# Down projection by one level of Strassen's algorithm, in three chunks of the depth

## The chip, the core and the metric

The kernel runs on one core of a Trainium2 chip. The metric is device time in microseconds (us), the median of several executions; lower is better. Besides the executions that are only timed, one is profiled, and all rows below come from that one.

## The reference, cut to what matters

The program is a trunk layer: a token mixer (a state-space branch and an mLSTM branch), then a feed-forward block. The change lies in the last matrix product of the feed-forward block.

```python
def channel_mixer(x, g_pre, g_post, w_gate, w_up, w_conv, b_conv, w_down):
    h = rmsnorm(x, g_pre)
    a = causal_dwconv(h @ w_gate, w_conv, b_conv)
    y = (jax.nn.gelu(a, approximate=True) * (h @ w_up)) @ w_down
    return x + rmsnorm(y, g_post)
```

There are 2048 tokens after the 16 meta tokens are dropped, D = 1024 and FFN_DIM = 2816, so the down projection is a 2048 x 2816 by 2816 x 1024 product, in float32 accuracy.

## The kernel before, in words

Every float32 product is made of three matmuls: each operand is split into a rounded part "hi" (ScalarE, ACT, a copy into the fp32r type) and a remainder "lo" (VectorE, DVE, a subtraction), and `mm3` (lines 155 to 158) or `mm3x` (160 to 163, the same with the group check off) adds hi*hi, hi*lo and lo*hi in PSUM. A matmul has a 128 x 128 stationary operand and up to 512 moving columns.

The order of the work on each engine is made by a scheduler when the program is built: it takes instructions in the order of the program as far as their inputs and buffers are there, and may move later ones ahead. All transfers are issued from the SP queue, in the order so found.

The stages around the change:

- **The gate and up products (FFN stage).** They are already done by one level of Strassen's algorithm, in two halves of the tokens, p = 0 and p = 1. `ops_first` (1050) and `ops_second` (1066) make the seven combinations of the moving operand from the normalised activations: `op_load` brings two of the four blocks for two of the four depth tiles (1 MB each, into a buffer of the tag `mk`, of which there are three), three subtractions form the combinations in place, and `op_split` (1045) makes hi and lo. The results lie in the buffers `t4(0)` to `t4(11)` and `q4(0)`, `q4(1)`, of which there is one each. `ffn_weights` (1131) loads the gate and up weights of one 128-column block m, forms the combinations `s1` to `s4` and splits seven of them with `put` (lines 1142, 1143). `ffn_unit` (1163) runs the seven products in the order 1, 6, 2, 7, 5, 4, 3 in the PSUM tiles A, B and C; DVE or ACT reads a sum out between two products that follow each other in the same tile (`u1`, `u2`, `u3`, lines 1184 to 1204). Then come the convolution (1220 to 1222), the GELU and the product, and `y` goes to the DRAM buffer `y_d` (1228). A halo of two columns is copied between the halves by GpSimd (POOL, line 1168).
- **Between the halves** (1236, 1237) the moving operands of p = 1 are made, in the same buffers as those of p = 0.
- **The down projection** (1245 to 1295). For each half `nh` of the 1024 output columns, all 22 depth tiles of `w_down` are loaded and split (1257 to 1265), 22 x 2 buffers of 512 columns in `t4(0)` to `t4(10)`. For each of 16 token tiles, `y` comes back from `y_d` in three pieces (1271), is split (1274, 1275) and used as the stationary operand: 22 x 3 matmuls of 512 columns in one PSUM tile. ACT sums the squares (1281); DVE multiplies by the gain `g4b`, and in the second half normalises, adds the residual `h1_d` (1291, 1294) and the result is stored (1295). `rstd_of` (101) takes the inverse root on POOL.

Of the kernel before, what the change touches and what calls it, by code (L numbers as in the profile page):

```python
# [49 lines left out]
def mixer_ffn_kernel(  # L50
# [32 lines left out]
    y_d = dp.tile([NF, 128, 2048], F32, name="y_d")  # L83
    win_d = dp.tile([8, 128, 512], F32, name="win_d")
# [947 lines left out]
    WX = (514, 512)  # L1032

    def op_load(p, hf, half):
        w = WX[p]
        t = mk_tile()[:, 0:4 * w].rearrange("p (k c) -> p k c", k=2)
        ks = slice(4 * half + 2 * hf, 4 * half + 2 * hf + 2)
        if p == 0:
            G.memset(t[:, :, 0:2], 0.0)
            P.dma_start(out=t[:, :, 2:2 * w], in_=h2_d[:, ks, 14:14 + 2 * w - 2])  # L1040
        else:
            P.dma_start(out=t, in_=h2_d[:, ks, 1040:1040 + 2 * w])
        return t[:, :, 0:w], t[:, :, w:2 * w]

    def op_split(op, p, hf, src):
        hi, lo = (o[:, 2 * hf:2 * hf + 2, 0:WX[p]] for o in op)
        S.activation(hi, src, AF.Copy)  # L1047
        V.tensor_tensor(lo, src, hi.bitcast(F32), ALU.subtract)  # L1048

    def ops_first(p):  # L1050

        op = {n: (t4(2 * i), t4(2 * i + 1)) for i, n in enumerate((1, 6, 2, 7))}
        for hf in range(2):
            b11, b12 = op_load(p, hf, 0)
            op_split(op[1], p, hf, b11)
            b21, b22 = op_load(p, hf, 1)
            E = V if p else G
# [3 lines left out]
            op_split(op[6], p, hf, b22)  # L1061
            op_split(op[2], p, hf, b21)
            op_split(op[7], p, hf, b12)
        return op

    def ops_second(p, op, last):

        op.update({5: (t4(8), t4(9)), 4: (t4(10), t4(11)), 3: last()})
        for hf in range(2):
            b11, b12 = op_load(p, hf, 0)  # L1070
            b21, b22 = op_load(p, hf, 1)
            V.tensor_tensor(b11, b12, b11, ALU.subtract)
            op_split(op[5], p, hf, b11)
            V.tensor_tensor(b12, b22, b11, ALU.subtract)
            V.tensor_tensor(b21, b21, b12, ALU.subtract)
            op_split(op[4], p, hf, b21)
            op_split(op[3], p, hf, b22)
# [33 lines left out]
    op0 = ops_first(0)  # L1111
# [19 lines left out]
    def ffn_weights(m):  # L1131

        wg = dw.tile([128, D], F32, tag="ws", name="wg")
        P.dma_start(out=wg, in_=w_gate[m])
        wu = dw.tile([128, D], F32, tag="ws", name="wu")
        P.dma_start(out=wu, in_=w_up[m])
        a11, a12, a21, a22 = wg[:, 0:512], wg[:, 512:D], wu[:, 0:512], wu[:, 512:D]
        out_ = {}

        def put(n, pl, tag, src):  # L1140
            t = pl.tile([128, 2, 512], F32R, tag=tag, name=f"w{n}")
            S.activation(t[:, 0], src, AF.Copy)  # L1142
            V.tensor_tensor(t[:, 1], src, t[:, 0].bitcast(F32), ALU.subtract)  # L1143
            out_[n] = t.rearrange("p a (k f) -> p a k f", k=4)

        s1 = du.tile([128, 512], F32, tag="s1", name="s1")
        s2 = du.tile([128, 512], F32, tag="s2", name="s2")
        s3 = du.tile([128, 512], F32, tag="s3", name="s3")
# [9 lines left out]
        s4 = du.tile([128, 512], F32, tag="s3", name="s4")  # L1158
        V.tensor_tensor(s4, a12, s2, ALU.subtract)
        put(3, dx, "w3", s4)  # L1160
        return out_

    def ffn_unit(p, m, op):
# [8 lines left out]
        def piece(p0, pn):  # L1172


            def prod(ps, n, first):
                for k in range(4):
                    mm3x(ps, wt[n][:, 0, k], wt[n][:, 1, k], op[n][0][:, k, p0:p0 + pn], op[n][1][:, k, p0:p0 + pn],
                         first and k == 0, k == 3)

# [4 lines left out]
            prod(A, 1, True)  # L1184
            S.activation(u1, A, AF.Copy)
            yield
            prod(B, 6, True)
            V.tensor_tensor(u2, B, u1, ALU.add)
            yield
            prod(A, 2, False)  # L1190
            S.activation(gp_[:, x0 + p0:x0 + p0 + pn], A, AF.Copy)
            yield
            prod(B, 7, False)
# [3 lines left out]
            prod(C, 5, True)  # L1197
            V.tensor_tensor(u3, C, u3, ALU.add)
            yield
            prod(B, 4, False)  # L1200
            V.tensor_tensor(u1, B, u1, ALU.add)
            yield
            prod(C, 3, False)
# [14 lines left out]
        for o0, o1 in ((0, xe), (xe, 1024)):  # L1218
            c = dx.tile([128, 514], F32, tag="cc", name="cc", bufs=3)[:, 0:o1 - o0]
# [10 lines left out]
    ops_second(0, op0, lambda: (q4(0), q4(1)))  # L1230
# [5 lines left out]
    op1 = ops_first(1)  # L1236
    ops_second(1, op1, lambda: (q4(0), q4(1)))
    for m in range(NF):
        ffn_unit(1, m, op1)
    phX.close()  # L1240
    el = pool(ctx, "el", bufs=2)
# [5 lines left out]
    g4b = el.tile([128, D], F32, name="g4b", bufs=1)  # L1247
    bcast_row(g4b, g_ffn_post)
    o4 = [t4(11).bitcast(F32), q4(0).bitcast(F32), q4(1).bitcast(F32), el.tile([128, 4, 514], F32, name="o4", bufs=1)]
    o0 = [o4[i // 4][:, i % 4, 0:512] for i in range(16)]  # L1250
    sq2 = [el.tile([128, 2], F32, name=f"sq_{i}", bufs=1) for i in range(16)]
    chunks = [(0, 8), (8, 8), (16, 6)]
    for nh in range(2):
        wd = {}
        for k in range(0, NF, 4):
            kn = min(4, NF - k)
            w_s = mk_tile()[:, 0:kn * 512].rearrange("p (a n) -> p a n", a=kn)
            P.dma_start(out=w_s, in_=w_down[k * 128:(k + kn) * 128, nh * 512:(nh + 1) * 512].rearrange(
                "(a p) n -> p a n", a=kn))
            for a in range(kn):  # L1260
                if a % 2 == 0:
                    t = t4((k + a) // 2)
                wh, wl = wd[k + a] = (t[:, a % 2 * 2, 0:512], t[:, a % 2 * 2 + 1, 0:512])
                S.activation(wh, w_s[:, a], AF.Copy)
                V.tensor_tensor(wl, w_s[:, a], wh.bitcast(F32), ALU.subtract)
        for i in range(16):
            ps = pst("ac", [128, 512])
            for k0, kn in chunks:
                r = "p (m t) -> p m t"
                ys = dw.tile([128, D], F32, tag="ws", name="ys")[:, 0:kn * 128]  # L1270
                P.dma_start(out=ys.rearrange(r, m=kn),
                            in_=y_d[k0:k0 + kn, :, i * 128:(i + 1) * 128].rearrange("m p t -> p m t"))
                yh, yl = (dw.tile([128, D], F32R, tag=tg, name="yhl")[:, 0:kn * 128] for tg in ("wh", "wl"))
                S.activation(yh, ys, AF.Copy)  # L1274
                V.tensor_tensor(yl, ys, yh.bitcast(F32), ALU.subtract)  # L1275
                yh, yl = yh.rearrange(r, m=kn), yl.rearrange(r, m=kn)
                for kk in range(kn):
                    k = k0 + kk
                    mm3(ps, yh[:, kk], yl[:, kk], wd[k][0], wd[k][1], k == 0, k == NF - 1)
            jk = el.tile([128, 512], F32, tag="jk", name="jk")  # L1280
            S.activation(jk, ps, AF.Square, accum_out=sq2[i][:, nh:nh + 1])
            if nh == 0:
                V.tensor_tensor(o0[i], ps, g4b[:, 0:512], ALU.mult)
            else:
                o1 = el.tile([128, 512], F32, tag="o1", name="o1")
# [88 lines left out]
```

## Time and profile before

| what | value |
|---|---|
| median of 3 executions (lowest, highest) | 2879.54 us (2877.54, 2880.41) |
| the profiled execution: its time, its span | 2886.44 us, 2884.7 us |
| PE busy, share of the span | 2794.8 us, 97% |
| DVE, ACT, POOL busy | 1798.8, 1047.4, 183.2 us |
| FFN stage, p = 1, and its boundary from p = 0 | about 1945 to 2381 us |
| down projection, first and last matmul | 2381.0 and 2877.3 us |

The span runs from the first to the last instruction of the profiled execution; its time as the other executions are timed is 1.7 us more. "Busy" is the time in which an engine has an instruction in work. Matmuls overlap in the pipeline, so that the length of one says less than the distance from one start to the next.

### The profile page before, as it was taken

The numbers are of one execution on the slowest core, as the hardware profiler recorded it, in microseconds if no ns is written. First come the engines' busy times: TensorE is split into PE (matmuls) and PEld (weight loads), VectorE is DVE, ScalarE is ACT, GpSimd is POOL, SyncE is SP. The second block draws the span as 40 slices with busy tenths as digits, with TensorE's granted clock in tenths as the row PEclk, the third lists the DMA queues.
The fourth block names the chain that finished last, engine by engine and source line by source line (L and its number), as shares of the span: only waits on it lengthen the run. The fifth ranks groups of instructions, "written<-read, shape, count | busy, mean of one in ns | idle before, by whom it ended". The sixth has DMA issues, their size and how long they took to land.

```text
span 2884.7 us, 41374 instructions
## 1 busy us (share of the span) xinstructions
PE 2794.8 (97%) x15654; PEld 2506.7 (87%) x15654; DVE 1798.8 (62%) x3508; ACT 1047.4 (36%) x1995; POOL 183.2 (6%) x257
## 2 busy tenths in 40 slices
PE   8999999999999999998779999998999999999999
PEld 8999999999999987776579999996888888888887
DVE  4638897377555465576777777788777774224333
ACT  6102233233443444434344444444444443223221
POOL 1000000000000000212310000001000000000000
PEclk9999999999999999999989999999999999999999
DMA  8334453211454564676746222224222235334553
GB/s 303 105 73 137 169 162 117 74 69 70 147 158 134 159 200 134 196 221 219 234 142 201 80 81 84 71 82 175 81 84 78 87 98 179 95 99 146 166 168 125
DMA packets 328442, 389.74 MB, mean 135 GB/s; under 512 B 41569, under 2 KB 230390, under 8 KB 328114
## 3 DMA queue, kind: packets, MB, share of 16 engines
q1 hardware_dynamic: 328242, 387.10, 41.9%
q8 instruction: 123, 2.02, 0.3%
q14 instruction: 77, 0.63, 0.1%
HBM read 282.90 MB, written 104.12 MB: 134 GB/s over the span
## 4 chain that ended last, share of the span: by engine, by line
PE 83%; DMA 7%; DVE 6%; issue 2%; ACT 1%; POOL 1%; SPq 0%; POOLq 0%; DVEq 0%; ACTq 0%
PE mm L158 9%; PE mm L156 9%; PE mm L157 9%; PE ac L157 8%; PE ac L158 8%; PE ac L156 8%; PE ac L162 5%; PE ac L163 5%; PE ac L161 5%; PE mm L163 4%; PE mm L162 4%; PE mm L161 4%; DMA mk<-h_d 1%; DMA wo_d<-W 1%; DMA h_d<-mk 1%
## 5 line engine op out<-in xcount | busy, mean ns | idle before, releaser
L158 PE MATMUL mm<-hTh,wl 128*128 128x410 f32 (+3 forms) x1216 | 430.4, 354 | 0.0
L156 PE MATMUL mm<-hTh,wh 128*128 128x410 f32 (+3 forms) x1216 | 429.4, 353 | 0.1
L157 PE MATMUL mm<-hTl,wh 128*128 128x410 f32 (+3 forms) x1216 | 427.2, 351 | 0.0
L1275 DVE TENSOR_TENSOR yhl<-ys,yhl 128x1024 fp32r<-128x1024 f32 (+1 forms) x96 | 109.1, 1137 | 293.7 <-ACT yhl L1274 293.7
L157 PE MATMUL ac<-t,yhl 128*128 128x512 f32 x704 | 278.5, 396 | 0.0
L158 PE MATMUL ac<-t,yhl 128*128 128x512 f32 x704 | 277.3, 394 | 0.0
L156 PE MATMUL ac<-t,yhl 128*128 128x512 f32 x704 | 276.6, 393 | 0.0
L161 PE MATMUL mm<-t,w 128*128 128x258 f32 (+2 forms) x792 | 254.6, 322 | 12.6 <-ACT w L1142 9.7
L161 PE MATMUL ac<-t,w 128*128 128x258 f32 (+2 forms) x792 | 255.0, 322 | 12.1 <-ACT t L1047 8.0
L162 PE MATMUL mm<-t,w 128*128 128x258 f32 (+2 forms) x792 | 255.1, 322 | 1.3 <-DVE t L1048 1.3
L162 PE MATMUL ac<-t,w 128*128 128x258 f32 (+2 forms) x792 | 254.9, 322 | 1.1 <-DVE t L1048 1.1
L163 PE MATMUL mm<-t,w 128*128 128x258 f32 (+2 forms) x792 | 253.6, 322 | 1.7 <-DVE w L1143 1.7
L163 PE MATMUL ac<-t,w 128*128 128x258 f32 (+2 forms) x792 | 254.7, 322 | 0.0
L140 ACT ACTIVATE wh<-ws 128x512 fp32r<-128x512 f32 (+1 forms) x176 | 124.5, 708 | 317.7 <-PE mm L157 139.3
L156 PEld LDWEIGHTS mm<-hTh,wh 128*128 128x128 f32 x1216 | 229.2, 188 | 3.2 <-DVE ev L351 0.8
L157 PEld LDWEIGHTS mm<-hTl,wh 128*128 128x128 f32 x1216 | 229.2, 189 | 2.6
L158 PEld LDWEIGHTS mm<-hTh,wl 128*128 128x128 f32 x1216 | 229.2, 189 | 2.4
L1274 ACT ACTIVATE yhl<-ys 128x1024 fp32r<-128x1024 f32 (+1 forms) x96 | 94.8, 988 | 350.6 <-PE ac L157 349.0
L1142 ACT ACTIVATE w<-s 128x512 fp32r<-128x512 f32 x176 | 110.3, 630 | 192.5 <-PE ac L163 112.3
L161 PEld LDWEIGHTS mm<-t,w 128*128 128x128 f32 x792 | 151.0, 191 | 25.6 <-ACT w L1142 9.9
L161 PEld LDWEIGHTS ac<-t,w 128*128 128x128 f32 x792 | 150.7, 190 | 25.1 <-ACT t L1047 8.3
L142 DVE TENSOR_TENSOR wl<-ws,wh 128x512 fp32r<-128x512 f32 (+1 forms) x112 | 104.5, 936 | 108.4 <-ACT wh L140 108.1
(448 smaller groups left out, 6180.2 us busy)
## 6 DMA issues: line engine op xcount, KB each, us to landing
ys<-y_d SPq DMA_DIRECT2D x64, 512.0 KB, 3.7
wg<-in_w_gate_dram SPq DMA_DIRECT2D x44, 512.0 KB, 4.8
wu<-in_w_up_dram SPq DMA_DIRECT2D x44, 512.0 KB, 3.9
gab_d<-ev SPq DMA_DIRECT2D x80, 205.0 KB, 2.2
ws<-in_w_m_dram SPq DMA_DIRECT2D x32, 512.0 KB, 4.0
ws<-in_w_out_dram SPq DMA_DIRECT2D x64, 256.0 KB, 3.0
gat<-gab_d SPq DMA_DIRECT2D x48, 256.0 KB, 3.6
ys<-y_d SPq DMA_DIRECT2D x32, 384.0 KB, 3.1
```

The lines of the kernel that those rows point to most:

```text
L140: S.activation(wh, ws, AF.Copy, scale=scale)
L142: V.tensor_tensor(wl, ws, wh.bitcast(F32), ALU.subtract)
L156: T.matmul(out=ps, lhsT=lh, rhs=rh, start=first, stop=False)
L157: T.matmul(out=ps, lhsT=lh, rhs=rl, start=False, stop=False)
L158: T.matmul(out=ps, lhsT=ll, rhs=rh, start=False, stop=last)
L161: T.matmul(out=ps, lhsT=lh, rhs=rh, start=first, stop=False, skip_group_check=True)
L162: T.matmul(out=ps, lhsT=lh, rhs=rl, start=False, stop=False, skip_group_check=True)
L163: T.matmul(out=ps, lhsT=ll, rhs=rh, start=False, stop=last, skip_group_check=True)
L1142: S.activation(t[:, 0], src, AF.Copy)
L1274: S.activation(yh, ys, AF.Copy)
L1275: V.tensor_tensor(yl, ys, yh.bitcast(F32), ALU.subtract)
```

## The change

The down projection is done by the same scheme as the gate and up products. The depth of 22 tiles is cut into three chunks of 6, 8 and 8 tiles (each two halves of 3, 4 and 4). In each chunk, blocks of `w_down` are the moving operands, made by the same `ops_first` and `ops_second` (both load the blocks anew), with the subtractions on DVE; pairs of token tiles of `y` are the stationary operands, made by `stationary`, which is `ffn_weights` without its loads. A chunk has eight units of seven products. The output of a unit is four tiles of 512 columns, `a`, in a buffer of the tag `mk`; it is stored to `acc_d` after the first chunk, loaded, added to and stored in the second, and loaded, added to and normalised in the third. The old functions are made general and keep their work; the buffer tag "cc" has four buffers in place of three, and the pools of the FFN stage stay open.

```diff
+    acc_d = dp.tile([8, 128, 2048], F32, name="acc_d")
...
+    def ops_first(load, nk, w, E):
 
         op = {n: (t4(2 * i), t4(2 * i + 1)) for i, n in enumerate((1, 6, 2, 7))}
+        for k in range(0, nk, 2):
+            n = min(2, nk - k)
+            b11, b12 = load(0, k, n)
+            op_split(op[1], w, k, n, b11)
+            b21, b22 = load(1, k, n)
             E.tensor_tensor(b11, b12, b11, ALU.subtract)
             E.tensor_tensor(b12, b22, b12, ALU.subtract)
             E.tensor_tensor(b22, b22, b11, ALU.subtract)
+            op_split(op[6], w, k, n, b22)
+            op_split(op[2], w, k, n, b21)
+            op_split(op[7], w, k, n, b12)
         return op
 
+    def ops_second(load, nk, w, op, last):
 
         op.update({5: (t4(8), t4(9)), 4: (t4(10), t4(11)), 3: last()})
+        for k in range(0, nk, 2):
+            n = min(2, nk - k)
+            b11, b12 = load(0, k, n)
+            b21, b22 = load(1, k, n)
             V.tensor_tensor(b11, b12, b11, ALU.subtract)
+            op_split(op[5], w, k, n, b11)
             V.tensor_tensor(b12, b22, b11, ALU.subtract)
             V.tensor_tensor(b21, b21, b12, ALU.subtract)
+            op_split(op[4], w, k, n, b21)
+            op_split(op[3], w, k, n, b22)
...
+    g4b = du.tile([128, 1028], F32, tag="gp", name="g4b")[:, 0:D]
     bcast_row(g4b, g_ffn_post)
-    for nh in range(2):
...
-        for i in range(16):
-            ps = pst("ac", [128, 512])
...
-                    mm3(ps, yh[:, kk], yl[:, kk], wd[k][0], wd[k][1], k == 0, k == NF - 1)
...
+    def wd_load(k0, nk):
+        def load(half, k, n):
+            t = mk_tile()[:, 0:n * D].rearrange("p (k c) -> p k c", k=n)
+            r0 = (k0 + half * nk + k) * 128
+            P.dma_start(out=t, in_=w_down[r0:r0 + n * 128, :].rearrange("(k p) n -> p k n", k=n))
+            return t[:, :, 0:512], t[:, :, 512:D]
+        return load
+
+    def y_pair(k0, nk, i):
+        yr = []
+        for half in range(2):
+            t = dw.tile([128, 4, 256], F32, tag="ws", name="yr")[:, 0:nk]
+            m0 = k0 + half * nk
+            P.dma_start(out=t, in_=y_d[m0:m0 + nk, :, i * 256:(i + 1) * 256].rearrange("m p t -> p m t"))
+            yr.append(t)
+        return stationary(yr[0][:, :, 0:128], yr[1][:, :, 0:128], yr[0][:, :, 128:256], yr[1][:, :, 128:256])
+
+    def down_unit(c, nk, wt, op, i):
+        a = mk_tile()[:, 0:2048].rearrange("p (a n) -> p a n", a=4)
+        if c:
+            P.dma_start(out=a.rearrange("p a n -> p (a n)"), in_=acc_d[i])
...
+        def more(j, u):
+            if c == 0:
+                return u
+            G.tensor_tensor(a[:, j], a[:, j], u, ALU.add)
+            return a[:, j]
+
+        prod(A, wt, op, 1, nk, pc, True)
+        S.activation(u1, A, AF.Copy)
+        prod(B, wt, op, 6, nk, pc, True)
+        V.tensor_tensor(u2, B, u1, ALU.add)
+        a12 = more(1, u2)
+        prod(A, wt, op, 2, nk, pc, False)
+        if c:
+            V.tensor_tensor(a[:, 0], A, a[:, 0], ALU.add)
+        else:
+            S.activation(a[:, 0], A, AF.Copy)
+        prod(B, wt, op, 7, nk, pc, False)
+        V.tensor_tensor(u3, B, u1, ALU.add)
+        a22 = more(3, u3)
+        a21 = more(2, u1)
+        C = pst("ac", [128, 512])
+        prod(C, wt, op, 5, nk, pc, True)
+        V.tensor_tensor(a[:, 3], C, a22, ALU.add)
+        prod(B, wt, op, 4, nk, pc, False)
+        V.tensor_tensor(a[:, 2], B, a21, ALU.add)
+        prod(C, wt, op, 3, nk, pc, False)
+        V.tensor_tensor(a[:, 1], C, a12, ALU.add)
+        if c < 2:
+            P.dma_start(out=acc_d[i], in_=a.rearrange("p a n -> p (a n)"))
+            return
+        for j in (1, 0):
...
+                P.dma_start(out=ht, in_=h1_d[NM + ts.start:NM + ts.stop, hh * 512:(hh + 1) * 512])
...
+                S.activation(jk, a[:, 2 * j + hh], AF.Square, accum_out=sq2[:, hh:hh + 1])
+                (V if i == 7 else G).tensor_tensor(a[:, 2 * j + hh], a[:, 2 * j + hh],
+                                                   g4b[:, hh * 512:(hh + 1) * 512], ALU.mult)
...
+            rs = rstd_of(dsm, sq, 128, 1, 1.0 / D)
+            for hh, ht in enumerate(hts):
+                V.scalar_tensor_tensor(ht, a[:, 2 * j + hh], rs, ht, ALU.mult, ALU.add)
+                P.dma_start(out=out[ts, hh * 512:(hh + 1) * 512], in_=ht)
+
+    for c, (k0, nk) in enumerate(((0, 3), (6, 4), (14, 4))):
+        ld = wd_load(k0, nk)
+        op = ops_first(ld, nk, 512, V)
+        ops_second(ld, nk, 512, op, lambda: (q4(0), q4(1)))
+        for i in range(8):
+            down_unit(c, nk, y_pair(k0, nk, i), op, i)
```

## Rows read from the trace of the kernel before

**Rows 1.** The page: busy time of PE, and shares of the last chain.

```profile
PE 2794.8 (97%) x15654; PEld 2506.7 (87%) x15654; DVE 1798.8 (62%) x3508; ACT 1047.4 (36%) x1995; POOL 183.2 (6%) x257
...
PE 83%; DMA 7%; DVE 6%; issue 2%; ACT 1%; POOL 1%; SPq 0%; POOLq 0%; DVEq 0%; ACTq 0%
```

**Rows 2.** Windows: us, PE, PEld, DVE, ACT, POOL busy (instructions), PEclk, DMA share, GB/s.

```profile
1953.00:1961.50 8.50, 0.49 (x1) 0.19 (x1) 7.38 (x12) 3.28 (x6) 6.38 (x1) 0.76 0.58 213
1961.50:1968.00 6.50, 6.49 (x16) 5.09 (x17) 6.50 (x7) 2.06 (x3) 0.00 (x0) 0.53 0.23 89
...
2100.00:2200.00 100.00, 100.00 (x432) 80.98 (x431) 73.43 (x116) 42.83 (x67) 6.08 (x5) 1.00 0.26 87
2381.00:2400.00 19.00, 19.00 (x83) 15.36 (x82) 16.31 (x25) 11.03 (x18) 0.49 (x1) 1.00 0.89 296
...
2500.00:2600.00 100.00, 100.00 (x432) 80.88 (x431) 26.26 (x26) 22.87 (x32) 0.00 (x0) 1.00 0.32 92
```

**Rows 3.** Groups by line: one of the three matmul lines of the down projection.

```profile
L157 PE MATMUL ac<-t,yhl 128*128 128x512 f32 x704 | 278.5, 396 | 0.0
```

**Rows 4.** Timeline of PE between the halves: the first and the last wait.

```profile
1946.16 0.50 PE L162 MATMUL mm<-t,w 128*128 128x512 f32 x1 [1.31 <-DVE t L1048]
...
1961.51 1.22 PE L161 MATMUL ac<-t,w 128*128 128x512 f32 x2 [8.01 <-ACT t L1047]
```

**Rows 5.** The chain in order of time, between the halves: start, us, what.

```profile
1918.89 0.44 DVE u L1201
...
1953.29 6.38 POOL gp L1168
```

**Rows 6.** Groups by line: operand splits of 1024 columns, and the normalising step of 512.

```profile
L1048 DVE TENSOR_TENSOR t<-mk,t 128x1024 fp32r<-128x1024 f32 x12 | 14.5, 1220 | 1.4 <-ACT t L1047 1.4
L1047 ACT ACTIVATE t<-mk 128x1024 fp32r<-128x1024 f32 x12 | 12.4, 1051 | 1.4 <-DVE mk L1060 1.2 <-DVE mk L1059 0.2
...
L1294 DVE SCALAR_TENSOR_TENSOR ht<-o,rs,ht 128x512 f32<-128x512 f32 x20 | 14.6, 747 | 2.9 <-POOL rs L105 2.9
```

**Rows 7.** Timeline of DVE with full work: start, us.

```profile
1956.53 1.22 DVE L1048 TENSOR_TENSOR t<-mk,t 128x1024 fp32r<-128x1024 f32 x1
1957.66 0.69 DVE L1143 TENSOR_TENSOR w<-wg,w 128x512 fp32r<-128x512 f32 x1
1958.26 0.69 DVE L1151 TENSOR_TENSOR s<-s,wg 128x512 f32<-128x512 f32 x1
```

**Rows 8.** DMA issues from 1900 to 2000 us: count, KB each, us to landing.

```profile
mk<-h_d SPq DMA_DIRECT2D x5, 1024.0 KB, 6.2
mk<-in_w_down_dram SPq DMA_DIRECT2D x3, 1024.0 KB, 4.9
wu<-in_w_up_dram SPq DMA_DIRECT2D x5, 512.0 KB, 4.0
```

**Rows 9.** Timelines of POOL and of DVE, where POOL adds tiles of 512 columns.

```profile
1190.25 3.44 POOL L1021 TENSOR_TENSOR o<-o,xh 128x512 f32<-128x512 f32 x2 [1.00 <-DVE o L1020]
...
1197.50 1.31 POOL L1021 TENSOR_TENSOR o<-o,xh 128x512 f32<-128x512 f32 x1 [0.72 <-DMA xh<-in_x_dram]
...
1190.82 1.73 DVE L142 TENSOR_TENSOR wl<-ws,wh 128x512 fp32r<-128x512 f32 x1
...
1195.57 1.77 DVE L142 TENSOR_TENSOR wl<-ws,wh 128x512 fp32r<-128x512 f32 x1
1198.73 0.69 DVE L142 TENSOR_TENSOR wl<-ws,wh 128x512 fp32r<-128x512 f32 x1 [1.40 <-ACT wh L140]
```

**Rows 10.** SP at the stores of y: waits in ns, min/median/max.

```profile
L1228 SPq EVENT_SEMAPHORE  x81: 17/17/10147, 1510.8 to 2371.7; - x81
```

**Rows 11.** Timeline of the end: last matmul, square, last stores.

```profile
2877.29 0.39 PE L158 MATMUL ac<-t,yhl 128*128 128x512 f32 x1
2877.71 0.60 ACT L1281 ACTIVATE jk<-ac 128x512 f32<-128x512 f32 x1 [9.14 <-PE ac L158]
...
2880.88 0.99 SPq L1295 DMA_DIRECT2D out_dram<-ht  x2
```

More of the change, by code (lines that the diff above doesn't have):

```diff
@@ L1026, in norm_block, with op_split @@
             norm_tile(mk_tile(), pl, blkC[b][0] + c0, rows)
[L1032 to L1046, printed above, removed]
+    def op_split(op, w, k, n, src):
+        hi, lo = (o[:, k:k + n, 0:w] for o in op)
         S.activation(hi, src, AF.Copy)
         V.tensor_tensor(lo, src, hi.bitcast(F32), ALU.subtract)
-    def ops_first(p):
+    def ops_first(load, nk, w, E):
         op = {n: (t4(2 * i), t4(2 * i + 1)) for i, n in enumerate((1, 6, 2, 7))}
[L1053 to L1057, printed above, removed]
+        for k in range(0, nk, 2):
[3 more added lines that the diff above has]
+            b21, b22 = load(1, k, n)
             E.tensor_tensor(b11, b12, b11, ALU.subtract)
@@ L1129, in mixer_ffn_kernel, with stationary @@
     dsm = Small(dx, "n", 2)
[L1131 to L1137, printed above, removed]
+    def stationary(a11, a12, a21, a22):
+        nk = a11.shape[1]
         out_ = {}
         def put(n, pl, tag, src):
[L1141 to L1148, printed above, removed]
+            t = pl.tile([128, 2, 4, 128], F32R, tag=tag, name=f"w{n}")
+            S.activation(t[:, 0, 0:nk], src, AF.Copy)
+            V.tensor_tensor(t[:, 1, 0:nk], src, t[:, 0, 0:nk].bitcast(F32), ALU.subtract)
+            out_[n] = t
+        s1, s2, s3 = (du.tile([128, 4, 128], F32, tag=f"s{i}", name=f"s{i}")[:, 0:nk] for i in (1, 2, 3))
         put(1, dw, "wh", a11)
@@ L1157, in ffn_weights @@
         put(4, dx, "w4", a22)
-        s4 = du.tile([128, 512], F32, tag="s3", name="s4")
+        s4 = du.tile([128, 4, 128], F32, tag="s3", name="s4")[:, 0:nk]
         V.tensor_tensor(s4, a12, s2, ALU.subtract)
@@ L1161, in ffn_weights, with prod @@
         return out_
+    def prod(ps, wt, op, n, nk, cols, first):
+        for k in range(nk):
+            mm3x(ps, wt[n][:, 0, k], wt[n][:, 1, k], op[n][0][:, k, cols], op[n][1][:, k, cols],
+                 first and k == 0, k == nk - 1)
+    def ffn_weights(m):
+        wg = dw.tile([128, D], F32, tag="ws", name="wg")
+        P.dma_start(out=wg, in_=w_gate[m])
+        wu = dw.tile([128, D], F32, tag="ws", name="wu")
+        P.dma_start(out=wu, in_=w_up[m])
+        h = lambda t, i: t[:, i * 512:i * 512 + 512].rearrange("p (k f) -> p k f", k=4)
+        return stationary(h(wg, 0), h(wg, 1), h(wu, 0), h(wu, 1))
     def ffn_unit(p, m, op):
@@ L1172, in piece @@
         def piece(p0, pn):
[L1175 to L1178, printed above, removed]
+            pc = slice(p0, p0 + pn)
             A, B = pst("ac", [128, pn]), pst("mm", [128, pn])
```

108 lines of the change are left out of this document (40 added, 68 removed).

## The prediction

> **What bounds the kernel now.** I read the page first: TensorE (PE) is busy for 97% of the span and carries 83% of the chain that ended last [rows 1]. Busy time alone proves little, so I went on to the windows. In the FFN stage of the second half and in the down projection PE starts 432 matmuls of 512 columns in every 100 us, at full granted clock [rows 2]: one start each 0.2315 us, the same for both forms. The down projection has three lines of 704 matmuls [rows 3], 2112 in all, 489 us at that distance, and first and last matmul lie 496 us apart with some 30 of the FFN's among them: nothing waits in it. DVE is busy there for only 26% of the time, against 73% in the FFN stage [rows 2]. So the down projection is bound by the count of its matmuls, and it has idle DVE time to give.
>
> The one place that shows what Strassen's scheme costs when its moving operands change is the boundary between the FFN halves. PE waits there five times, 1.31 us at first and 8.01 us last [rows 4], 11.4 us together; then the granted clock is 0.53 (mostly the lower level, 1.2 GHz) and 16 matmuls take 6.5 us in place of 3.7 [rows 2]. The boundary costs 11.4 + 2.8 = 14.2 us. The chain shows why: DVE carries it from 1918.9 us on, and at the end a POOL copy of two columns takes 6.38 us because it cannot get in beside DVE [rows 5].
>
> **The sum, part by part.** The profiled execution took 2886.4 us (span 2884.7), 6.9 above the median of 2879.5; I apply differences to the median.
>
> *Matmuls.* Eight units x 7 products x 3 x depth tiles (3 + 4 + 4) are 1848. 264 fewer x 0.2315 = **-61.1 us**. A unit lasts 63 x 0.2315 = 14.6 us in the first chunk and 84 x 0.2315 = 19.4 in the others, if PE never waits.
>
> *Inside the units.* DVE with full work starts one 1024-column instruction every 1.13 us and one of 512 columns every 0.60 [rows 7]. A unit of the second chunk has 7 splits, 4 combinations and 6 sums out of PSUM: 17 x 0.60 = 10.2 us of DVE in 19.4; the first chunk has less of both (5 PSUM sums, 11 instructions of 384 columns). The FFN stage runs the same order of products with 73 us of DVE in 100 and no wait, so this is hidden. The third chunk adds per unit 4 normalising steps at 0.75 [rows 6] and small ones, 0.6: 13.8 us.
>
> POOL is new here: three additions per unit in the second chunk, three additions and four multiplications in the third. A POOL addition of 512 columns takes 1.31 us, and a DVE split that meets one takes 1.73 or 1.77 us instead of 0.69 [rows 9]: DVE loses 1.05. In the second chunk that makes 10.2 + 3 x 1.05 = 13.4 us of 19.4: nothing. In the third, 13.8 + 7 x 1.05 = 21.1 if every one meets DVE, 13.8 if none does. The ends are 0 and 8 x (21.1 - 19.4) = 13 us; most meet DVE's idle time or a PSUM read, so **+3**. (The Trainium skill, "SBUF — State Buffer", section Who interferes with whom, says that a DVE instruction with two SBUF inputs and a POOL one that reads SBUF exclude each other for a whole instruction. By it DVE would lose the full 1.31 us and the high end would be 8 x (23.0 - 19.4) = 29; the trace agrees in kind, at 1.05 each.)
>
> *First boundary (FFN to chunk 1).* Each chunk remakes its moving operands in the same single buffers, so operand n can be written only when product n of the last old unit is done. The nearest row is the boundary of the halves. Without its POOL copy, which has no counterpart, 14.2 - 6.4 = 7.8. Operands of depth 4 take 26 DVE instructions of 1024 columns, 26 x 1.13 = 29.4 us; depth 3 takes 13 x (1.13 + 0.60) = 22.5, 6.9 less, while the products of depth 3 end 6 x 0.69 = 4.1 earlier. **+5.** The three `mk` buffers are free there, so the first blocks of `w_down` come early.
>
> *Second boundary (chunk 1 to 2).* Here the `mk` buffers are not free: they hold the sums `a` of the last units until they are stored. Count from the start of the last old unit, 1 MB taking 4.9 us [rows 8]. The buffer of unit 6 is stored at about 5, and the second block of the first pair is there at 10. Then come three subtractions (3.4), and splits 6, 2, 7, one ACT copy (1.05 [rows 6]) and three DVE instructions (3.4): 17.9. Only then is a buffer free for the second pair, loaded at 22.8 and split for product 1 at 25. PE has finished the old unit at 14.6 and the half of product 1 that it can do at 16: it loses 9. Product 6 needs three more subtractions and a split after 25, at 30.6, against 27.8: 2.8. The second set (5, 4, 3) loads four blocks again through the same buffers and is late by 2.7 and 2.5; products of the next unit can fill about half of that. The low clock costs 2.8, and DVE's regular work between (some 25 us in these 47) pushes 3 more: **+20**. POOL's additions wait behind DVE here, and DVE's own `a[:, 3]` waits for one; that is in the 3.
>
> *Third boundary (chunk 2 to 3).* The same with a last unit 4.9 us longer, so that the first loss is 4 instead of 9: **+16**. For each of these two, the ends are 7.8 (as the first form, buffers never late) and 29.4 + 2 x 6.2 = 41.8 us (all DVE work and two loads at the slower landing of [rows 8] in the open); I stand nearer the low one, since PE ran on through most of the DVE work in the boundary that the trace shows.
>
> *Transfers.* Token tiles are read once instead of twice, `w_down` twice instead of once, and `a` goes out twice and in twice: 8 x 4 MB. In all about 97 MB in place of 74, over some 480 us about 200 GB/s; the trace moves 296 GB/s between 2381 and 2400 us without a PE wait [rows 2]. SP issues 168 transfers for 156. A store of `a` waits on SP for the last sum of its unit, and the loads of `y` and `a` for later units stand behind it; the FFN's stores hold SP for up to 10.1 us [rows 10] and PE does not stop. Hidden: **0**, with the loads at the boundaries already counted.
>
> *End.* From the last matmul to the end of the span are 7.4 us [rows 11]. A sum out of PSUM comes before the square; the gain multiplication now runs beside the square instead of after it. **+0.5.**
>
> Sum: -61.1 + 3 + 5 + 20 + 16 + 0.5 = -16.6; 2879.5 - 16.6 = **2863 us**.
>
> **Rivals.** *A, the boundaries are cheap.* Buffers come free early and the two later boundaries cost 7.8 each, the third chunk nothing: -61.1 + 5 + 15.6 + 0.5 = -40, 2839.5 us. For it: PE waited for only 11.4 us of some 40 in which DVE led [rows 4, 5], and products of two units can mix. Against it: three `mk` buffers for both blocks and sums.
>
> *B, POOL and DVE bound the third chunk.* All seven POOL operations meet DVE (13), and a PSUM tile is read one POOL operation late in each unit (8 x 1.31 = 10.5). 24 in place of 3: +4, 2883.5 us: no change. Against it: 5.6 us of DVE idle per unit.
>
> *C, slower: the boundaries take back more than the matmuls give.* One mechanism, the three `mk` buffers: loads start only when sums are stored and pairs are split, nothing of the next unit moves up, and DVE, waiting, has its regular work still to do after. Then the second boundary costs 9 + 2.8 + 5.2 + 2.8 + 10 = 30, the third 26, the first the full 14.2: -61.1 + 70 + 3 + 0.5 = +12.6, 2892 us. It decides from 58 us on for the three together.
>
> That the matmuls do not become fewer or come at another distance can be left out: the FFN has this very form at 432 per 100 us [rows 2].
>
> **How the numbers follow.** Forecast 0.45, A 0.30, B 0.10, C 0.15. The measurement can tell about 0.2%, 5.8 us, from no change: below 2873.8 is faster, above 2885.3 slower. Faster: 0.42 of the forecast, 0.30, 0.01: 0.73. Same: 0.03 + 0.05 + 0.02 = 0.10. Slower: 0.04 of B, 0.13 of C: 0.17. The range runs from just beyond A (2836) to just beyond C (2896). The forecast's own range, from its boundaries 10 us cheaper or dearer, is 2853 to 2873.
>
> **What would show it.** Right: 1848 matmuls after the FFN, 432 per 100 us inside the chunks; PE waits in three clusters, at about 117 and 290 us after the first chunk starts the larger ones, released by ACT or DVE splits of `w_down` blocks behind DMA waits; SP or DVE waiting for stores of `acc_d`. A: clusters under 10 us. B: PE waits spread over all eight units of the third chunk, DVE near 100% there, and many DVE records of 1.7 us. C: clusters near 30 us. The forecast is wrong if PE waits inside the units of the first two chunks, or if loads of `a` release PE.

## The result, and the profile after

The changed kernel takes 2906.8 us (four executions, 2899.1 to 2911.6) beside 2880.0 us of the kernel before on the same chip: 1.0091 times as long, 95% interval 1.0067 to 1.0115. It is slower by some 26 us; 2863 was predicted, with 2836 to 2896 as range: the time lies above the range. The profiled execution took 2899.05 us (span 2897.3).

The page of the changed kernel, busy time and the chain (before: [rows 1]):

```profile
PE 2757.4 (95%) x15390; PEld 2461.3 (85%) x15390; DVE 2003.7 (69%) x3818; ACT 1085.4 (37%) x2097; POOL 303.1 (10%) x333
...
PE 73%; DVE 10%; DMA 9%; issue 3%; POOL 2%; ACT 1%; SPq 0%; DVEq 0%; POOLq 0%; ACTq 0%
```

264 matmuls are gone, as counted. But PE's busy time falls by 37 us only, its share of the chain by 10 points, and DVE's and DMA's shares rise. Where PE waits is read from the windows (columns as in [rows 2]): inside chunk 1, at the second boundary (two windows), at the third, and over four units of the third chunk.

```profile
2420.00:2500.00 80.00, 78.92 (x339) 63.06 (x338) 47.72 (x89) 28.06 (x53) 0.00 (x0) 1.00 0.38 137
2500.00:2520.00 20.00, 10.92 (x43) 7.63 (x41) 18.75 (x27) 7.38 (x10) 0.00 (x0) 0.88 0.66 246
2520.00:2560.00 40.00, 34.16 (x133) 25.52 (x134) 32.68 (x35) 15.47 (x19) 7.04 (x5) 0.93 0.62 221
2700.00:2750.00 50.00, 40.23 (x142) 29.67 (x143) 40.63 (x47) 18.79 (x29) 15.15 (x11) 0.86 0.63 225
2767.00:2855.00 88.00, 80.72 (x336) 62.40 (x336) 69.57 (x101) 30.37 (x64) 51.72 (x37) 1.00 0.56 192
```

88 us would hold 380 matmuls at 0.2315 us each; the third chunk starts 336. DVE has 19 of 20 us of work where PE does worst.

For the table below I went through PE's timeline and added up, from each start to the next, what lies beyond 0.2315 us per matmul (all 1848 of the down projection have a record; where one stage is cut from the next moves an entry by 2 to 3 us). The kernel before loses next to nothing from 1970 us on. Between kernels whose edits lie behind it, the first boundary came out at 12 to 19 us, and the third chunk, where its own work was not edited, at 17 to 22: smaller differences than these say nothing.

| TensorE time lost, us | first boundary | chunk 1 and second boundary | chunk 2 and third boundary | third chunk | last matmul to end |
|---|---|---|---|---|---|
| predicted | 5 | 20 | 16 | 3 | 7.9 |
| changed kernel | 12 | 24 | 28 | 19 | 9.6 |

-61.1 + 83 + 2 = +24 us, which agrees with the ratio. The two spans differ by less (12.6 us): the profiled execution before was 6.9 us above its median, the one after is 7.8 below its own.

**Second boundary.** The chain in order of time (start, us, what) shows one buffer of the tag `mk` passing on: sums out, block in, split, combine.

```profile
2513.10 4.75 DMA acc_d<-mk
2517.86 4.71 DMA mk<-in_w_down_dram
2522.60 1.07 ACT t L1035
2523.69 1.24 DVE t L1036
2524.95 1.24 DVE mk L1046
2526.21 1.23 DVE mk L1047
...
2532.61 6.78 DMA mk<-in_w_down_dram
2539.41 1.22 DVE mk L1063
```

PE's longest wait stands there, and another at the third boundary:

```profile
2518.75 0.79 PE L162 MATMUL mm<-t,w 128*128 128x512 f32 x1 [6.41 <-ACT t L1035]
...
2690.33 0.77 PE L162 MATMUL ac<-q,w 128*128 128x512 f32 x1 [3.99 <-DVE mk L1314]
```

**Third boundary.** That second wait is not for an operand. DVE's timeline shows the reading of a PSUM tile (L1314) queued behind subtractions, the first of which had to wait for a block of `w_down`:

```profile
2686.02 1.23 DVE L1047 TENSOR_TENSOR mk<-mk 128x1024 f32<-128x1024 f32 x1 [3.37 <-DMA mk<-in_w_down_dram]
2687.16 1.29 DVE L1147 TENSOR_TENSOR w<-s,w 128x512 fp32r<-128x512 f32 x2
2688.36 1.22 DVE L1048 TENSOR_TENSOR mk<-mk 128x1024 f32<-128x1024 f32 x1
2689.50 0.68 DVE L1314 TENSOR_TENSOR mk<-ac,mk 128x512 f32<-128x512 f32 x1
```

**Third chunk.** From the third unit on every unit waits about 1.5 us at its head, where the new unit's products and the old unit's last steps meet. PE, DVE and POOL around one such place, and on DVE a pair of normalising steps (L1338) some us later that meets no POOL operation, and two of DVE's waits for products, behind that:

```profile
2812.93 0.50 PE L162 MATMUL mm<-t,w 128*128 128x512 f32 x1 [1.51 <-DVE u L1301]
...
2806.94 2.96 DVE L1338 SCALAR_TENSOR_TENSOR ht<-mk,rs,ht 128x512 f32<-128x512 f32 x2
2809.82 1.79 DVE L1147 TENSOR_TENSOR w<-s,w 128x512 fp32r<-128x512 f32 x1
2811.53 0.68 DVE L1152 TENSOR_TENSOR s<-yr 128x512 f32<-128x512 f32 x1
...
2816.96 1.41 DVE L1338 SCALAR_TENSOR_TENSOR ht<-mk,rs,ht 128x512 f32<-128x512 f32 x2
...
2825.22 0.69 DVE L1316 TENSOR_TENSOR mk<-mm,mk 128x512 f32<-128x512 f32 x1 [1.97 <-PE mm L164]
...
2828.48 0.69 DVE L1318 TENSOR_TENSOR mk<-ac,mk 128x512 f32<-128x512 f32 x1 [1.43 <-PE ac L164]
...
2807.92 1.43 POOL L1332 TENSOR_TENSOR mk<-mk,g4b 128x512 f32<-128x512 f32 x1 [0.26 <-ACT jk L1331]
2809.31 1.74 POOL L1295 TENSOR_TENSOR mk<-mk,u 128x512 f32<-128x512 f32 x1
```

Two normalising steps that take 1.41 us elsewhere take 2.96 beside POOL, and a split 1.79 instead of 0.68; the read of PSUM (L1301) comes behind them. POOL is an obvious suspect, and the first experiment takes its work away from it.

### The profile page after: what moved, and what is told of

It reads as the page before. It is cut to its first block, busy times and chain, and to the rows that moved or that the text cites. A ratio compares the mean times of both kernels' runs of the same rounds, so it can differ in the third digit from the quotient of the medians.

```text
span 2897.3 us, 41382 instructions
## 1 busy us (share of the span) xinstructions
PE 2757.4 (95%) x15390; PEld 2461.3 (85%) x15390; DVE 2003.7 (69%) x3818; ACT 1085.4 (37%) x2097; POOL 303.1 (10%) x333
## 4 chain that ended last, share of the span: by engine, by line
PE 73%; DVE 10%; DMA 9%; issue 3%; POOL 2%; ACT 1%; SPq 0%; DVEq 0%; POOLq 0%; ACTq 0%
PE mm L159 9%; PE mm L157 9%; PE mm L158 9%; PE ac L162 6%; PE ac L164 6%; PE ac L163 6%; PE mm L162 5%; PE mm L163 5%; PE mm L164 5%; PE ac L158 3%; PE ac L157 3%; PE ac L159 3%; DMA mk<-in_w_down_dram 1%; DVE w L1147 1%; DMA mk<-h_d 1%
## 5 line engine op out<-in xcount | busy, mean ns | idle before, releaser
L162 PE MATMUL mm<-t,w 128*128 128x512 f32 (+2 forms) x1056 | 361.2, 343 | 37.7 <-DVE u L1301 13.1
L162 PE MATMUL ac<-t,w 128*128 128x512 f32 (+2 forms) x1056 | 364.2, 346 | 29.0 <-ACT t L1035 11.6
L163 PE MATMUL mm<-t,w 128*128 128x512 f32 (+2 forms) x1056 | 360.2, 341 | 5.6 <-DVE t L1036 5.6
L163 PE MATMUL ac<-t,w 128*128 128x512 f32 (+2 forms) x1056 | 362.8, 344 | 2.6 <-DVE t L1036 2.6
L164 PE MATMUL ac<-t,w 128*128 128x512 f32 (+2 forms) x1056 | 360.5, 343 | 1.5 <-DVE w L1147 1.5
L164 PE MATMUL mm<-t,w 128*128 128x512 f32 (+2 forms) x1056 | 357.8, 340 | 1.7 <-DVE w L1147 1.7
L1146 ACT ACTIVATE w<-s 128x512 fp32r<-128x512 f32 (+1 forms) x272 | 166.7, 617 | 310.7 <-PE ac L164 159.4
L162 PEld LDWEIGHTS mm<-t,w 128*128 128x128 f32 x1056 | 201.3, 191 | 70.4 <-DVE u L1301 17.6
L162 PEld LDWEIGHTS ac<-t,w 128*128 128x128 f32 x1056 | 202.0, 191 | 62.0 <-ACT t L1035 13.9
L163 PEld LDWEIGHTS mm<-t,w 128*128 128x128 f32 x1056 | 201.2, 190 | 30.0 <-DVE t L1036 7.7
L163 PEld LDWEIGHTS ac<-t,w 128*128 128x128 f32 x1056 | 202.9, 192 | 27.5 <-DVE t L1036 4.6
L164 PEld LDWEIGHTS ac<-t,w 128*128 128x128 f32 x1056 | 202.5, 192 | 26.1 <-DVE w L1147 2.9
L164 PEld LDWEIGHTS mm<-t,w 128*128 128x128 f32 x1056 | 200.3, 190 | 25.4 <-DVE w L1147 2.2
L1147 DVE TENSOR_TENSOR w<-s,w 128x512 fp32r<-128x512 f32 (+1 forms) x272 | 194.5, 717 | 15.4 <-ACT w L1146 15.2
```

Source lines behind the costliest of these rows:

```text
L162: T.matmul(out=ps, lhsT=lh, rhs=rh, start=first, stop=False, skip_group_check=True)
L163: T.matmul(out=ps, lhsT=lh, rhs=rl, start=False, stop=False, skip_group_check=True)
L164: T.matmul(out=ps, lhsT=ll, rhs=rh, start=False, stop=last, skip_group_check=True)
L1146: S.activation(t[:, 0, 0:nk], src, AF.Copy)
L1147: V.tensor_tensor(t[:, 1, 0:nk], src, t[:, 0, 0:nk].bitcast(F32), ALU.subtract)
```

## The experiments

All ratios are to the kernel before, run beside it on the same chip.

### POOL's work to DVE; the sums in buffers of their own; no third boundary; two of these together

`e1_dve_adds`:

```diff
-            G.tensor_tensor(a[:, j], a[:, j], u, ALU.add)
+            V.tensor_tensor(a[:, j], a[:, j], u, ALU.add)
...
-                (V if i == 7 else G).tensor_tensor(a[:, 2 * j + hh], ...
+                V.tensor_tensor(a[:, 2 * j + hh], ...
```

> The changed kernel with the additions and the gain multiplications of its units on DVE instead of POOL; the same sums. Changed kernel: 2907 us; its PE loses about 12 us in the boundary before the first chunk, 23 and 27 in the two later ones, 18 in the units of the third chunk. Theory 1 (the port that DVE and POOL share lengthens DVE's instructions, so that PSUM sums are read late): the third chunk's 18 us fall to 5 or less, the boundaries stay, 2890 to 2896 us. Rival (DVE simply has too much to do in the third chunk): DVE gets 4.2 us more per unit, 18 of 19.4, and the units lose as much or more, 2905 to 2925 us.

Ratio 1.0065 (1.0040 to 1.0089); the third chunk still loses 19 us. Its window over four units, beside that of the changed kernel above:

```profile
2770.00:2858.00 88.00, 80.94 (x336) 64.02 (x336) 70.89 (x129) 29.94 (x64) 5.63 (x8) 0.98 0.57 190
```

DVE runs 28 instructions more in nearly the same busy time: what POOL did for it, POOL's interference took away again. So the loss does not need POOL's additions and multiplications. What their absence would give if DVE did not get its work is not shown. The waits have moved to another place. DVE, ACT and PE at the head of a unit in this kernel:

```profile
2834.46 0.68 DVE L1318 TENSOR_TENSOR mk<-ac,mk 128x512 f32<-128x512 f32 x1
...
2835.24 0.63 ACT L1331 ACTIVATE jk<-mk 128x512 f32<-128x512 f32 x1 [0.18 <-DVE mk L1318]
2835.77 0.19 ACT L1331 ACTIVATION_READ_ACCUMULATOR jk<-mk 128x1 f32 x1
2835.87 0.58 ACT L1299 ACTIVATE u<-ac 128x512 f32<-128x512 f32 x1
...
2836.50 0.50 PE L162 MATMUL ac<-t,w 128*128 128x512 f32 x1 [2.11 <-ACT u L1299]
```

The next unit's first product had long been done; its reading on ACT (L1299) stood behind the square of the old unit's last sum.

`e2_sums_apart`: in chunks 1 and 2 each sum has a buffer of 512 columns (the tag `cc`) and is stored as soon as it is done.

```diff
-        a = mk_tile()[:, 0:2048].rearrange("p (a n) -> p a n", a=4)
...
+        if c < 2:
+            a = {}
+            for j in (0, 3, 2, 1):
+                a[j] = dx.tile([128, 514], F32, tag="cc", name="acc", bufs=4)[:, 0:512]
...
```

> The changed kernel with the sums of chunks 1 and 2 in the four buffers of the tag cc, stored and loaded tile by tile, so that the three mk buffers are free for blocks of w_down at all boundaries; the same sums. Theory 1 (the blocks come late because the mk buffers hold sums): the two later boundaries fall from 23 and 27 us to about 12 each, like the first, 2882 to 2888 us. Rival (the DVE work of the operands itself sets them): they fall by under 6 us together, 2901 us or more.

Ratio 1.0040 (1.0025 to 1.0054). Second boundary 24 to 17 us, third 28 to 24. So the shared buffers are a part, and not the larger one.

`e3_keep_operands`: `if c < 2:` ahead of `ops_first` and `ops_second`.

> The changed kernel without remaking the moving operands for the third chunk: it multiplies with those of the second chunk, so eight block loads, 12 subtractions and 14 splits of 1024 columns are left out (the output of that chunk is another). Both theories: the boundary of 27 us all but goes, at most 3 us left, 2880 to 2885 us. If the wait there came from the partial sums loaded back instead, some 10 us would stay, 2890 us.

Ratio 0.9982 (0.9969 to 0.9995). The third boundary falls from 28 us to 1, the third chunk still loses 17: these are two separate losses. With no boundary before it, the third chunk's first three units lose 0.1, 0.1 and 0.2 us, the fourth 1.9, the next three 2.6 to 2.8 each: the loss sets in only after some units, as if a start with work in hand hid it at first.

`e4_both` joins the first two edits.

> Both edits: sums apart from the blocks in chunks 1 and 2, and all additions and multiplications on DVE. If both theories hold, boundaries of about 12 us each and little in the units: the sum is 2907 - 25 - 13 = 2869 us, range 2864 to 2876, faster than before (2880). If DVE becomes the bound, 2885 to 2905 us.

Ratio 1.0036 (1.0024 to 1.0049), as with the sums apart alone: second boundary 16, third 24, third chunk 21. POOL's work on DVE adds nothing to it.

### Parts left out, or moved in the queues

`e5_late_epilogue`: the normalising loop becomes a function that the next unit calls behind `a21 = more(2, u1)`.

> Changed kernel, but in the third chunk the normalising steps of a unit are written in the program behind the fourth product of the next unit, not at the unit's own end. In the changed kernel the eight units of the third chunk lost 18.9 us, most of it as one wait of 1.5 to 2.1 us at the head of each unit, and so did they (18.7 us) without POOL's work. Theory 1 (order: the first reads of PSUM of the next unit stand on ACT and DVE behind the squares and normalising steps of the old one): the third chunk loses at most 5 us, the time is about 14 us below the changed kernel's, ratio to before 1.003 to 1.006. Rival (DVE has too much work there): it loses 15 us or more wherever the steps are written, ratio 1.008 to 1.010.

Ratio 1.0100 (1.0085 to 1.0115): no better, third chunk 23 us (25 by its last six units, as an expectation below counts it), end 13.5. SP stood at a store of the output for 11 us with the loads of `y` behind it, and DVE then waited for `y`:

```profile
2843.69 0.69 DVE L1152 TENSOR_TENSOR s<-yr 128x512 f32<-128x512 f32 x1 [4.06 <-DMA yr<-y_d]
```

`e6_no_epilogue`: the third chunk ends with `P.dma_start(out=out[ts, :], in_=a[:, 2 * j:2 * j + 2]...)`.

> Changed kernel, but the third chunk stores its sums as they are: squares, gain, root, normalising and the residual with its loads are left out. The additions to the loaded sums stay. If the normalising steps alone make the third chunk lose (by their order or by their amount), it loses at most 3 us in place of 18.9, the end after the last matmul falls from 9.6 to about 5 us, and the time is some 20 us below the changed kernel's: ratio to before 1.001 to 1.004. Rival (the loads of the sums and the additions do it): it still loses 10 us or more, ratio 1.005 or above.

Ratio 0.9974 (0.9964 to 0.9985). The third chunk loses 1 us and the end takes 5.3, as expected; POOL's three additions per unit are still there. What I had not expected: the third boundary falls too, from 28 to 18 us. The normalising steps, with POOL's multiplications and the loads of the residual that are left out with them, cost 18 + 10 + 4 = 32 us of path. For the residual itself no engine waits between 2767 and 2855 us of the changed kernel; its loads still stand in SP's queue.

`e7_sums_by_pool_queue`: `G.dma_start` for loads and stores of `acc_d`.

> Changed kernel, but stores and loads of the partial sums are issued by POOL's queue; the loads of y and w_down stay alone with the last stores on SP. In the changed kernel SP issued loads of sums for 12 us at a stretch at the second boundary (waiting for buffers), and loads of y stood behind them. Theory 1 (the order of SP's queue holds the loads of y and w_down back): the second boundary falls from 24 to 18 us or less, the third from 27 to 21 or less, the time by some 12 us: ratio to before 1.004 to 1.006. Rival (the three buffers and DVE hold them, whoever issues): both stay within 3 us, ratio 1.008 to 1.011; POOL's additions may come later behind its waiting stores and cost some us more.

Ratio 1.0086 (1.0067 to 1.0106): second boundary 26, third 29. SP's order was not it.

`e8_no_combinations`: `if comb:` ahead of the subtractions in `ops_first` and `ops_second`, off in the down projection.

> Changed kernel, but the six subtractions per pair of depth tiles that combine blocks of w_down are left out; every operand is still split. That takes 12 of 26 DVE instructions of 1024 columns, 13.6 of 29.4 us, from each of the last two boundaries, and no load. Theory 1 (DVE's work at the boundaries holds PE): first boundary 12.6 to 8 us, second 24 to 16, third 27 to 18, some 21 us less in all: ratio to before 1.000 to 1.004. Rival (loads of w_down and the buffers hold PE): the three together fall by less than 9 us, the second stays at 20 or more, ratio 1.006 to 1.010.

Ratio 0.9967 (0.9954 to 0.9980). First boundary 12 to 1 us, second 24 to 18, third 28 to 12. The subtractions are the largest part of the three boundaries together, and at the first nearly the whole; the gain is larger than expected.

### The combinations made ahead

`e9_late_pool_queue`: the late steps again, with `G.dma_start` for the residual and the output.

> The kernel with the late normalising steps, whose third chunk lost 24.9 us, with the loads of the residual and the stores of the output issued by POOL's queue. In that kernel SP stood for 11 us at a store that waited for DVE, with the loads of the residual and of y behind it, and DVE and ACT waited 4 to 9 us per unit for y. Theory 1 (y late behind SP's waiting stores, no lack of DVE time): the third chunk loses 8 us or less, ratio to before 1.002 to 1.006. Rival (DVE and ACT have too much in their queues, y is only the last to be late): it loses 16 us or more, ratio 1.007 to 1.011.

Ratio 1.0096 (1.0081 to 1.0111). Third chunk 14 us (17 by its last six units), between the two theories or at the edge of the rival; the end grew to 20.4, and the ratio is the rival's.

`e10_combinations_ahead`: 

```diff
+    def combine(q):
...
+        V.tensor_tensor(b11, b12, b11, ALU.subtract)
+        V.tensor_tensor(b12, b22, b12, ALU.subtract)
+        V.tensor_tensor(b22, b22, b11, ALU.subtract)
+        V.tensor_tensor(b21, b21, b22, ALU.subtract)
+        for half in range(2):
+            P.dma_start(out=cmb_d[q, half, :, 0:n * D], in_=ts[half])
     for m in range(NF):
         ffn_unit(1, m, op1)
+        if m % 3 == 1 and m < 18:
+            combine(m // 3)
...
```

> Changed kernel, but the combinations of w_down for all three chunks are made by DVE during the second half of the FFN stage (22 subtractions of 1024 columns and 2 per shorter pair at 512, about 25 us, four per pair of depth tiles since two of the six repeat each other) and stored to DRAM; at the boundaries seven blocks of 512 columns are loaded per pair and only split. Same result as the changed kernel. Theory 1 (the combinations on DVE are the larger part of the boundaries, and the FFN stage with DVE busy 73% of its time hides 25 us more): as without combinations, the losses fall from 88 to about 57 us, ratio 0.996 to 0.999. Rival (the FFN stage cannot hide them): it loses 10 us or more there, ratio 1.000 to 1.004.

Ratio 0.9964 (0.9949 to 0.9979): with the same computation as the changed kernel, faster than both. First boundary 1, second 10, third 11; the FFN stage loses 14 us more, its longest wait

```profile
2006.34 0.50 PE L163 MATMUL ac<-t,w 128*128 128x512 f32 x1 [2.04 <-ACT w L1147]
```

where the first combinations come. Both theories hold in part, and the gain is the larger.

`e11_ahead_sums_apart` adds the edit of `e2_sums_apart`.

> Combinations made ahead, and the sums of chunks 1 and 2 in buffers of their own, so that the three large buffers serve the blocks of w_down alone. If buffers and DVE's combinations are two separate parts of the boundaries, the second and third lose 4 to 8 us less each than with the combinations ahead alone: ratio 0.992 to 0.996. If they are the same part (once the combinations are gone, the blocks come early enough), the two kernels differ by less than 4 us: ratio 0.996 to 0.999.

Ratio 0.9950 (0.9935 to 0.9965). Second boundary 10 to 2 us: there buffers and combinations were separate parts, by the trace; the intervals of the two ratios overlap. Its window in place of the one with 10.92 us of PE above:

```profile
2500.00:2520.00 20.00, 20.00 (x88) 16.25 (x87) 17.61 (x28) 12.13 (x21) 0.00 (x0) 1.00 0.47 155
```

`e12_ahead_late` adds the late steps and POOL's queue.

> Combinations ahead, sums apart, normalising steps written half a unit later and the residual and output on POOL's queue: all in one. If each part acts for itself, the first two boundaries together lose 20 us or less, the third 12 or less, the third chunk 8 or less: ratio 0.988 to 0.992. If the third chunk is bound by DVE's amount of work, it still loses 16 us or more and the ratio stays at 0.993 to 0.997.

Ratio 0.9969 (0.9956 to 0.9982): third chunk 30 us instead of 22, end 15.5.

### The third chunk

The base of these is `e11_ahead_sums_apart`, whose third chunk, cut in the same place of the work, loses 22 us (14.9 in expectations below, which count from a later unit on).

`e13_half_late`: only the steps of sums 0 and 1 go behind the next unit's reads.

```diff
+        post(1)
+        return post
...
         a12 = more(1, u2)
+        if before:
+            before(0)
```

> Combinations ahead, sums apart, and in the third chunk the squares, gains and normalising steps of the first token tile of a unit (sums 0 and 1, of which sum 1 is the unit's last) are written behind the first two reads of PSUM of the next unit; those of the second tile stay at the unit's end. Theory 1 (the first reads stand behind the steps that wait for the unit's last sum): the third chunk falls from 14.9 to 6 us or less, ratio to before some 0.003 below the 0.995 of the base: 0.990 to 0.993. Rival (y late, or too much work): 11 us or more, ratio 0.994 to 0.997.

Ratio 0.9939 (0.9924 to 0.9954), 2865.5 us, the lowest ratio of the kernels with the whole result; the interval overlaps that of the base. The third chunk loses 15 us: better, but between the theories.

`e14_late_two_y`, `e15_half_late_two_y`, `e16_two_y`: `spare = mk_tile() if k0 == 14 and i % 2 else None` for the pair of `y` tiles.

> Combinations ahead, sums apart, all normalising steps half a unit later, and every second pair of y tiles in one of the large buffers, so that y of the next unit can be loaded while that of this one is in use. If y was late for lack of a buffer, the third chunk loses 6 us or less (22.8 with one pair), ratio 0.990 to 0.993. If SP's queue holds y behind waiting stores all the same, it loses 15 us or more, ratio 0.995 to 0.998.

> Combinations ahead, sums apart, the steps of the first token tile late, and two pairs of buffers for y. If both the place of the steps and the buffer of y count, the third chunk loses 4 us or less, ratio 0.989 to 0.992; if only the place counts, as with the steps half late alone; if DVE has too much work, 11 us or more, ratio 0.994 to 0.997.

> Combinations ahead, sums apart, and two pairs of buffers for y in the third chunk, nothing else. If the place of the steps makes the loss, nothing changes: third chunk 13 to 16 us, ratio 0.994 to 0.996. If y late makes it, 6 us or less, ratio 0.990 to 0.993.

Ratios 0.9980 (0.9971 to 0.9989), 0.9966 (0.9953 to 0.9978), 0.9978 (0.9966 to 0.9991); third chunk 20, 17 and 24 us. A second pair of buffers for `y`, taken from the three of the tag `mk`, helps in none. Whether the late `y` of `e5_late_epilogue` was a cause or a consequence is not shown: in `e14_late_two_y` ACT still waits for `y` for 23 us between 2740 and 2850 us, and SP stands at stores of the output for up to 19.

`e17_no_y_sums`: in the third chunk `s1, s2, s3, s4` are `a21, a22, a21, a12`.

> Combinations ahead, sums apart (third chunk lost 14.9 us), and in the third chunk the four sums of y tiles that form the stationary operands are left out; each operand is still split. That is 4 of some 23 DVE instructions per unit, 2.4 of 17.4 us; normalising steps, loads and places are as they were. Theory 1 (DVE's amount of work in each unit): the third chunk loses 6 us or less and the ratio falls from 0.995 to 0.989 to 0.992. Rival (the first reads of a unit stand behind the squares and normalising steps that wait for the last sum): each unit still waits 1.5 us or more at its head, third chunk 12 us or more, ratio 0.993 to 0.996.

Ratio 0.9939 (0.9926 to 0.9953), but the third chunk loses 22 us as before, though DVE is busy 54 of 80 us in place of 62 (the base first):

```profile
2768.00:2848.00 80.00, 74.67 (x308) 57.74 (x306) 61.52 (x90) 26.73 (x57) 43.60 (x31) 0.99 0.52 171
2768.00:2848.00 80.00, 72.95 (x286) 55.91 (x285) 54.42 (x75) 25.89 (x57) 44.33 (x35) 0.94 0.45 155
```

But these are not the waits of the base. With the sums left out, all seven operands are split from the `y` tiles themselves, which are needed until the last split, and the next `y` comes late. PE now waits for a split on ACT, and ACT for `y`, 23 us in this window for 4 in the base's:

```profile
2816.86 1.67 ACT L1147 ACTIVATE w<-yr 128x512 fp32r<-128x512 f32 x3 [5.91 <-DMA yr<-y_d]
...
2817.54 0.50 PE L163 MATMUL ac<-t,w 128*128 128x512 f32 x1 [2.30 <-ACT w L1147]
```

So the run changes two things, and what less DVE work alone does stays open.

`e18_y_sums_ahead`: these four sums made in the first chunk, stored to DRAM and loaded in the third, with the edit of `e13_half_late`.

> Combinations of w_down ahead, sums apart, last two normalising steps of a unit late (ratio 0.994 so far, third chunk 13.2 us), and the four sums of y for the third chunk made by DVE during the first chunk, stored, and loaded again: 1 MB more written and read per unit. Same result as the changed kernel. If DVE's amount of work is what the third chunk lacks, it loses 6 us or less, the first chunk 3 or less, ratio 0.988 to 0.992. If the further load per unit comes late through the large buffers, the third chunk waits for it, 12 us or more, ratio 0.993 to 0.997.

Ratio 0.9959 (0.9946 to 0.9973). In the third chunk PE is busy 78 of 80 us (first line below) and loses 6 us in all. The gain is lost elsewhere: the second boundary loses 9 us (2 in `e13_half_late`), and the third 18 (7 there), where the added load comes late; its chain, and PE's wait:

```profile
2768.00:2848.00 80.00, 78.03 (x335) 62.50 (x334) 57.89 (x84) 27.90 (x62) 43.62 (x37) 1.00 0.69 243
...
2682.94 8.50 DMA mk<-cmb_d
...
2693.80 7.79 DMA mk<-ysum_d
...
2702.30 0.79 PE L164 MATMUL mm<-t,w 128*128 128x512 f32 x1 [14.14 <-ACT w L1148]
```

The four runs side by side, all with the normalising steps kept: base 22 us lost; half of the steps in another place (`e13_half_late`) 15; less DVE work, but `y` late (`e17_no_y_sums`) 22; half of the steps in another place and less DVE work (`e18_y_sums_ahead`) 6. The wait of 14 us ahead of the last could hide a loss at first, as in `e3_keep_operands`; but its last four units too lose 4 us for the base's 13.

## Why the prediction was wrong

**Matmuls, -61.1: right.** 15,390 for 15,654, and at the old distance inside chunks 1 and 2.

**"Inside the units", third chunk +3: the step that failed.** Measured 19 us. The forecast missed by 44 us: 16 of them here, 12 at the third boundary, 7 at the first, 4 at the second, 2 at the end, the rest within the error of the table. I compared DVE's sum of work with a unit's length, found 13.8 to 21.1 of 19.4 us, and took what is left as cover. DVE was indeed busy only 70 of 88 us. But its idle time lies in the middle of the unit, where it waits for products, while the steps cluster at the unit's head together with the reads of PSUM on which PE waits. Rival B named the right place and nearly the right size (24), by POOL's operations meeting DVE's; `e1_dve_adds` shows that the loss stays when POOL's work is on DVE, `e6_no_epilogue` that it goes with the normalising steps. What in them does it stays open: half of them in another place took 22 us to 15, with less DVE work besides to 6; but `e18_y_sums_ahead` changes loads too, less DVE work has no run of its own in which `y` came in time, and steps moved as a whole (`e5_late_epilogue`, `e9_late_pool_queue`, `e12_ahead_late`) gave 14 to 30 us with no rule that I could see.

**Third boundary +16: measured 28.** Without the normalising steps it is 18, near the term (whose parts add up to 15), but not by its mechanism: buffers of their own for the sums took only 4 us off (`e2_sums_apart`), the subtractions left out 16 (`e8_no_combinations`). What it left out is that the first units of the third chunk bring their squares and normalising steps into the time when DVE makes operands; I had charged that work to the chunk's inside alone.

**First boundary +5: measured 12** (to 19 in other kernels). The step that failed is the subtraction of 6.9 us for the smaller depth: it took DVE's saved work off the loss one for one, from a row at which PE ran through most of that work; without it the same sum gives 11.9. `e8_no_combinations` and `e10_combinations_ahead` show that the loss needs DVE's subtractions: 1 us without them.

**Second boundary +20: measured 24,** by the mechanism foretold: store, load, split, with the 6.4 us wait for the first split of a block. The buffers are worth 7 us (`e2_sums_apart`) and, with the combinations gone, another 8 (`e11_ahead_sums_apart`).

**Transfers 0: right** for the queue (`e7_sums_by_pool_queue`). **End +0.5: measured +2.2:** a gain multiplication (L1332, at 2887.90 us) stands on DVE ahead of the last sum (L1318, at 2888.50), and the square follows that; no run tests it.

Rival C came nearest, 2892, with 70 us for the three boundaries against 64 measured; but its mechanism, the three buffers, carries only a part of it, so its size was in part luck. The 58 us it gave as deciding were passed, and the third chunk's loss came on top. B and C were priced as alternatives, and the range ended just beyond C; their terms together, -61.1 + 70 + 24 + 0.5 = +33, give 2913 us.

## What to carry to other kernels

A scheme that saves matmuls by combining operands pays at every place where the operands change: count the work of the combining engine there as path, and if it depends on inputs alone, do it earlier, under a stage with idle time (here 36 us, from 1.0091 to 0.9964). Free time in the sum is no proof of cover: DVE, busy for 79% of a unit, cost TensorE 19 us here, where its work and the reads that PE waits for stand in the same few microseconds. Whether their place or their amount decides is open here; a forecast has to look at both. When steps are moved from a stage with one kind of slack to another, price them at the boundary as well as inside.

## What the runs showed of the hardware

POOL's help can be worth nothing: 28 instructions moved from POOL to DVE left DVE's busy time over 88 us at 70.9 us against 69.6, because beside POOL a pair of normalising steps took 2.96 us for 1.41 and a split 1.79 for 0.68. And a wait can cost more than its length: behind some of them PE runs at the lower of its two clocks, while behind the waits of 1.5 us in the third chunk the granted clock stays at 1.00 (2767 to 2855 us). In the changed kernel the granted clock is 0.86 from 2700 to 2750 us (window above), and after one wait, where the granted clock is 0.50, the timeline of PE shows starts 0.43 us apart in place of 0.23:

```profile
2579.93 0.80 PE L162 MATMUL ac<-t,w 128*128 128x512 f32 x1 [1.96 <-ACT w L1146]
2580.52 0.63 PE L163 MATMUL ac<-t,w 128*128 128x512 f32 x1
2580.95 0.63 PE L164 MATMUL ac<-t,w 128*128 128x512 f32 x1
...
2580.00:2582.00 2.00, 2.00 (x5) 1.57 (x6) 1.21 (x3) 0.00 (x0) 0.71 (x1) 0.50 0.61 220
```
